# The experts' stage as one written stream of weight pieces, and six low parts moved from GpSimd to VectorE

## The chip, the cores and the metric

The kernel runs on one core of a Trainium2 chip. The metric is the device time of one execution in microseconds (us). A profiled execution also has a span, from its first to its last instruction.

Engines are named as in the profile: PE is TensorE's matmul, PEld its weight load, DVE is VectorE, ACT ScalarE, POOL GpSimd, SP SyncE. Each takes its instructions in order; SP and POOL also issue DMA transfers.

## The reference

The input of 1024 tokens of 1024 values goes through two blocks. The change lies in the first block's last part, a mixture of 16 experts in which each expert chooses its own tokens:

```python
def expert_choice_ffn(h, w_router, w_gate, w_up, w_down):
    cap = CAPACITY_FACTOR * seq // N_EXPERTS                 # 2 * 1024 // 16 = 128
    probs = softmax(einsum('bld,de->ble', h, w_router))
    gate, idx = lax.top_k(transpose(probs, (0, 2, 1)), cap)  # 128 tokens per expert
    xs = h[idx]                                              # (16, 128, 1024)
    a = einsum('becd,edf->becf', xs, w_gate)                 # w_gate, w_up: 16 x 1024 x 2048
    u = einsum('becd,edf->becf', xs, w_up)
    y = einsum('becf,efd->becd', silu(a) * u, w_down)        # w_down: 16 x 2048 x 1024
    y = y * gate[..., None]
    return segment_sum(y, idx)                               # added back to the tokens' rows
```

Before it stand a norm, a gated mixer and a state-space branch; after it a second block with attention, a recurrence and a last norm. All weights are float32.

## The kernel before

**Split products.** A float32 matrix product is made of three products in the fast float32 form. Each operand is split into a high part (a rounded copy) and a low part (what the copy leaves over), and `mm3` (L240) adds high x high, high x low and low x high. A weight piece is 128 rows of 1024 columns. `piece` (L1845) makes its high part on ScalarE (L1849) and its low part by a subtraction (L1853). The high parts are named wh and mh, the low parts wl and ml, for even and odd pieces; each name has three buffers, so there are six pairs. The subtraction runs on GpSimd for the first six pieces of the stage and on VectorE for all others. ScalarE's first six copies stand behind the router's last exponential (`k.route`).

**Loads.** `fetched` (L1825) loads two pieces, 1 MB, at a time, into a ring of large buffers (eight A, two pairs of wr, two mr; at the stage's start two more pairs, t and m). SP issues these loads, and a load waits until the low parts of the buffer's earlier content are made. The loads numbered 15 and 16 are issued by GpSimd, ordered behind the first gather of rows (`k.rows`).

**One expert.** `gather` (L1856) finds the expert's token numbers: VectorE compares slot numbers (the one-hot oh, L1859), eight small matmuls sum it, ScalarE and VectorE make the index (L1868, L1869; the first is `k.first`), and GpSimd fetches the 128 rows by an indirect DMA (L1876). `transposed` (L1882) turns the rows by TensorE (L228), and evicts them as a high part on ScalarE (L1890) and a low part on VectorE (L1891). The hidden width of 2048 is made in two halves, the units u = (expert, half). For a unit come three products of eight pieces: `gate`, `up` and `down`. A piece is six matmuls of 512 columns. `up` starts with the silu of the gate sums on ScalarE (L1925) and ends with the product of the two on VectorE (L1929). `flip` transposes that into the operand of `down`. After the second half's `down`, ScalarE scales the sums by the router's weight (L1949), and GpSimd adds the rows to the tokens by an indirect DMA that accumulates (L1950), the scatter. The last expert's rows are taken over by the second block instead (`k.tail`).

**Order.** The loop at the end of `moe` traces `up(u)`, `gate(u + 1)`, `down(u)` for each unit, with the index work of the next expert ahead of `up`, the transposes of its rows ahead of `up`'s seventh piece, and `flip(u)` ahead of `gate(u + 1)`'s seventh piece. Splits are traced just ahead of their matmuls. The program's compile-time planner then orders each engine's instructions: it plays the program through with estimated durations, and takes the first traced one among those it holds ready. `add_manual_dep` with ORDER adds an edge to this planning and no wait on the chip. In `_pe` (L230) such edges keep the matmuls that write one accumulation tile in their order. The router (`Router`, L1389) ends just ahead of the stage: a sort by eight maxima at a time (L1461, L1463), merges of sorted rows (L1487, L1488), a threshold, then the slots (L1551).

Of the kernel before, what the change touches and what calls it, by code (L numbers as in the profile page):

```python
# [13 lines left out]
OP = mybir.AluOpType  # L14
# [140 lines left out]
class K:  # L155
    def __init__(s, tc, ins, ctx):
        s.tc, s.nc, s.i, s.ctx = tc, tc.nc, ins, ctx
        s.pp = ctx.enter_context(tc.tile_pool(name="pp", bufs=8, space=PSUM))
        s.dp = ctx.enter_context(tc.tile_pool(name="dp", bufs=1, space=DRAM))
        s.base = ctx.enter_context(tc.tile_pool(name="base", bufs=1))  # L160
        s.pool = s.base
        s.n = 0
        s.spare = {}
        s.last = {}
        s.turn = False
        s.wait = None

    def nm(s, p):
        s.n += 1
# [60 lines left out]
    def _pe(s, out, x):  # L230
        n = out.tensor.name
        if n in s.last:
            s.tc.add_manual_dep(x.ins, s.last[n].ins.name, ORDER, reason="one group of a bank at a time")
        s.last[n] = x
        if s.wait:
            s.tc.add_manual_dep(x.ins, s.wait.ins.name, ORDER, reason="what is surely ready first")
            s.wait = None
        s.pe = x
# [1572 lines left out]
def moe(k, dbg=None):  # L1811
    nc, i, c = k.nc, k.i, k.c
    V, S, SY, GP = nc.vector, nc.scalar, nc.sync, nc.gpsimd
    dbg = dbg or {}
    ident = c("ident")
    PM = k.tc.tile_pool(name="PM", bufs=1)
    k.pool = PM.__enter__()
    NE, NF = 16, 2048
    cnt = [0]

    turns = ["A"] * 8 + ["wr"] * 2 + ["mr"] * 2
    first = ["A"] * 8 + ["t"] + ["wr"] * 2 + ["mr"] * 2 + ["m"]
    MH, AHEAD = 3, 2

    def fetched(src):  # L1825
        n = cnt[0] // 2

        q = first[n] if n < len(first) else turns[(n - len(first)) % len(turns)]
        if q in ("A", "mr"):
            z = k.a2(F32) if q == "A" else k.t([128, 2048], "mr", 2)  # L1830
            to = [(z, src)]
            got = [z[:, :1024], z[:, 1024:]]
        else:
            got = [k.wraw(), k.wraw()] if q == "wr" else [k.g("th"), k.g("tl")] if q == "t" else [k.m(5), k.m(4)]
            to = list(zip(got, (src[:, :1024], src[:, 1024:])))
        for z, x in to:
            if n in (len(first) + 1, len(first) + 2):

                x = GP.dma_start(z, x)
                k.tc.add_manual_dep(x.ins, k.rows.ins.name, ORDER, reason="the rows first")  # L1840
            else:
                SY.dma_start(z, x)
        return got

    def piece(raw):  # L1845
        n = cnt[0]
        cnt[0] += 1
        h, l = (k.g("wh", k.NH, FR, k.base), k.g("wl", k.NH, FR, k.base)) if n % 2 == 0 else (k.g("mh", MH, FR), k.g("ml", MH, FR))
        a = S.activation(h, raw, AF.Copy)  # L1849
        if n < 6:  # L1850

            k.tc.add_manual_dep(a.ins, k.route.ins.name, ORDER, reason="routing first")
        (GP if n < 6 else V).tensor_tensor(l, raw, h, op=OP.subtract)  # L1853
        return h, l

    def gather(e):  # L1856
# [3 lines left out]
        if e == 1:  # L1860
            k.tc.add_manual_dep(x.ins, k.first.ins.name, ORDER, reason="the first expert first")
# [6 lines left out]
        S.activation(a, p[:, 0:1], AF.Copy, scale=8.0)  # L1868
# [24 lines left out]

    def product(w, x, first, last, ps, before=None):

        for kk in range(8):
            if kk % 2 == 0:
                raw = fetched(w[kk // 2])
            wh, wl = piece(raw[kk % 2])
            if kk == 8 - AHEAD and before:  # L1900
                before()
            xs = slice(kk * 128, kk * 128 + 128)
            for h in range(2):
                hs = slice(h * 512, h * 512 + 512)
                k.mm3(ps[h], x[0][:, xs], x[1][:, xs], wh[:, hs], wl[:, hs], first and kk == 0, last and kk == 7)

    X, hid, G, Dn = {}, {}, {}, {}
    units = [(e, h) for e in range(NE) for h in range(2)]

    def fetch(e):  # L1910
        X[e] = gather(e)

    def turn(e):
        X[e] += (transposed(X[e][1], "x", 2),)

    def gate(u, before=None):
        e, h = units[u]
        G[u] = [k.ps("pa") for _ in range(2)]
        product(i["w_gate"][e, h], X[e][2], True, True, G[u], before)

    def up(u, before=None):
        e, h = units[u]
        g = k.m(2 + u % 2)
        for q in range(2):
            S.activation(g[:, q * 512:(q + 1) * 512], G[u][q], AF.Silu)  # L1925
        P = [k.ps("pa") for _ in range(2)]
        product(i["w_up"][e, h], X[e][2], True, True, P, before)
        for q in range(2):
            V.tensor_tensor(g[:, q * 512:(q + 1) * 512], g[:, q * 512:(q + 1) * 512], P[q], op=OP.mult)  # L1929
        hid[u] = g  # L1930

    def flip(u, tag="t"):
        hid[u] = transposed(hid[u], tag, 1 if tag == "t" else 2)

    def down(u):
        e, h = units[u]
        x = hid[u]
        if h == 0:
            Dn[e] = [k.ps("pb") for _ in range(2)]
        product(i["w_down"][e, h], x, h == 0, h == 1, Dn[e])  # L1940
        if h == 1:
            ix, xs, _ = X[e]
            if e == NE - 1:

                k.tail = ix, xs[:, 1024 + e:1025 + e], Dn[e]
                return
            y = k.m(4 + e % 2)
            for q in range(2):
                S.activation(y[:, q * 512:(q + 1) * 512], Dn[e][q], AF.Copy, scale=xs[:, 1024 + e:1025 + e])  # L1949
            GP.indirect_dma_start(out=k.acc[:, :], out_offset=bass.IndirectOffsetOnAxis(ap=ix[:, :1], axis=0),  # L1950
                                  in_=y, in_offset=None, compute_op=OP.add)

    fetch(0)
    turn(0)
    gate(0)
    n = len(units)
    for u in range(n - 1):
        e, h = units[u]
        if h == 0 and e + 1 < NE:
            fetch(e + 1)  # L1960

        up(u, (lambda: turn(e + 1)) if h == 1 and e + 1 < NE else None)
        gate(u + 1, lambda: flip(u))
        if u + 2 < n:
            down(u)
    up(n - 1)
    flip(n - 1, "x")
    down(n - 2)
    down(n - 1)
    PM.__exit__(None, None, None)  # L1970


# [22 lines left out]
```

## Time and profile before

| | us |
|---|---|
| median of 3 runs | 2871.28 (2870.67 to 2875.26) |
| the profiled execution | 2875.23 |
| its span | 2873.5 |
| PE busy | 2763.0 (96%) |
| PEld busy | 2253.5 (78%) |
| DVE busy | 2232.4 (78%) |
| ACT busy | 1618.4 (56%) |
| POOL busy | 138.4 (5%) |

Matmuls are pipelined and their ends are modelled, so a busy PE is not necessarily a PE at its peak. The starts of neighbouring matmuls tell more. Busy shares are means over stages with different limits. In a timeline row an instruction's start and duration stand first; what its engine waited for just before it stands in brackets at the end.

### The profile page before, as it was taken

Reading aid. Unit: us, or ns where it says so; the run is one execution under the profiler, and the core shown is the slowest. Engines: PE = TensorE matmul, PEld = TensorE weight load, DVE = VectorE, ACT = ScalarE, POOL = GpSimd, SP = SyncE. Lnnn points to the kernel's source line nnn. Section 1 sums busy time; section 2 is a strip of 40 time slices with the busy share of each in tenths; the row PEclk is TensorE's granted clock in tenths of the full one; section 3 lists DMA queues with packets and bytes.
Section 4 is the critical chain, followed back from the end, with each engine's and each line's share of the span. In section 5 each row is a group of like instructions: output and inputs, shape, how many; then the busy total and the mean of one; then the engine's idle time right before and its main releaser. Section 6 shows DMA issues by size and latency. Waiting matters only on the chain. (4 is left out here: it accounts for less than half of the span.)

```text
span 2873.5 us, 37166 instructions
## 1 busy us (share of the span) xinstructions
PE 2763.0 (96%) x13353; PEld 2253.5 (78%) x13353; DVE 2232.4 (78%) x3619; ACT 1618.4 (56%) x2205; POOL 138.4 (5%) x106
## 2 busy tenths in 40 slices
PE   8999999949999999999999998899999999999998
PEld 8889887738888877777777776688888788887877
DVE  7966476679999888888888888978888565568774
ACT  6343234228888777777777776546655344445531
POOL 0000000020000000000000001200000300000000
PEclk9999999979999999999999999899999999999999
DMA  7223465459999999999999996123334754457762
GB/s 257 67 75 96 132 215 187 169 195 339 375 379 375 354 364 365 365 364 364 366 364 365 365 367 212 54 105 112 114 129 143 232 152 161 158 203 261 259 202 81
DMA packets 181705, 678.18 MB, mean 236 GB/s; under 512 B 34960, under 2 KB 46352, under 8 KB 140816
## 3 DMA queue, kind: packets, MB, share of 16 engines
q1 hardware_dynamic: 176624, 656.80, 62.8%
q0 software_dynamic: 4896, 19.01, 2.6%
q8 instruction: 105, 1.72, 0.2%
q14 instruction: 80, 0.66, 0.1%
HBM read 588.01 MB, written 85.62 MB: 234 GB/s over the span
## 5 line engine op out<-in xcount | busy, mean ns | idle before, releaser
L225 PE MATMUL ps<-A,wh 128*128 128x512 f32 x1920 | 603.6, 395 | 4.5 <-DVE u L541 1.9
L225 PEld LDWEIGHTS ps<-A,wh 128*128 128x128 f32 x1920 | 357.1, 188 | 81.9 <-issue 2.6
L225 PE MATMUL ps<-A,wl 128*128 128x512 f32 x960 | 375.9, 392 | 0.0
L1853 DVE TENSOR_TENSOR wl<-A,wh 128x1024 fp32r<-128x1024 f32 x253 | 308.8, 1221 | 38.5 <-ACT wh L1849 36.9
L1853 DVE TENSOR_TENSOR ml<-A,mh 128x1024 fp32r<-128x1024 f32 x253 | 308.5, 1219 | 9.5 <-ACT mh L1849 3.1
L225 PE MATMUL ps<-S,wh 128*128 128x512 f32 x960 | 304.4, 398 | 5.5 <-DVE u L546 3.4
L1849 ACT ACTIVATE wh<-A 128x1024 fp32r<-128x1024 f32 x256 | 270.2, 1055 | 23.9 <-PE ps L225 23.9
L1849 ACT ACTIVATE mh<-A 128x1024 fp32r<-128x1024 f32 x256 | 270.0, 1055 | 21.2 <-PE ps L225 21.1
L219 ACT ACTIVATE wh<-wr 128x512 fp32r<-128x512 f32 (+2 forms) x168 | 154.8, 922 | 223.5 <-PE ps L225 174.4
L225 PE MATMUL ps<-wl,xh 128*128 128x512 f32 x520 | 209.1, 402 | 10.1 <-DVE wl L1853 10.1
L220 DVE TENSOR_TENSOR wl<-wr,wh 128x1024 fp32r<-128x1024 f32 (+2 forms) x166 | 175.4, 1056 | 53.1 <-ACT wh L219 38.4
L225 PEld LDWEIGHTS ps<-S,wh 128*128 128x128 f32 x960 | 178.9, 189 | 45.7 <-DVE u L546 5.1
L225 PEld LDWEIGHTS ps<-A,wl 128*128 128x128 f32 x960 | 180.2, 188 | 39.6 <-issue 0.7
L225 PE MATMUL ps<-wh,xl 128*128 128x512 f32 x520 | 205.3, 395 | 0.0
L225 PE MATMUL ps<-ml,xh 128*128 128x512 f32 x520 | 204.1, 393 | 0.5 <-DVE ml L1853 0.5
L225 PE MATMUL ps<-mh,xl 128*128 128x512 f32 x520 | 203.3, 391 | 0.0
L225 PE MATMUL ps<-S,wl 128*128 128x512 f32 x480 | 189.1, 394 | 0.0
L225 PE MATMUL ps<-wh,xh 128*128 128x512 f32 x520 | 188.2, 397 | 0.0
L225 PE MATMUL ps<-mh,xh 128*128 128x512 f32 x520 | 186.6, 393 | 0.2 <-ACT mh L1849 0.2
L225 PE MATMUL ps<-wh,A 128*128 128x256 f32 (+1 forms) x704 | 143.5, 299 | 8.7 <-ACT wh L219 8.7
L228 PE MATMUL ps<-sm,m 128*128 128x128 f32 (+1 forms) x692 | 102.4, 278 | 28.6 <-DVE m L1488 14.2
L225 PEld LDWEIGHTS ps<-wl,xh 128*128 128x128 f32 x520 | 97.9, 188 | 39.9 <-DVE wl L1853 18.5
(509 smaller groups left out, 5505.7 us busy)
## 6 DMA issues: line engine op xcount, KB each, us to landing
A<-in_w_up_dram SPq DMA_DIRECT2D x125, 1024.0 KB, 7.9
A<-in_w_down_dram SPq DMA_DIRECT2D x65, 1024.0 KB, 6.8
A<-in_w_gate_dram SPq DMA_DIRECT2D x64, 1024.0 KB, 6.6
wr<-in_w_gate_dram SPq DMA_DIRECT2D x124, 512.0 KB, 7.0
mr<-in_w_down_dram SPq DMA_DIRECT2D x59, 1024.0 KB, 7.0
wr<-in_w_in_dram SPq DMA_DIRECT2D x82, 512.0 KB, 4.2
wr<-in_w_mod_dram SPq DMA_DIRECT2D x24, 512.0 KB, 4.4
wr<-in_w_ing_dram SPq DMA_DIRECT2D x16, 512.0 KB, 4.6
```

The lines of the kernel that those rows point to most:

```text
L219: s.parts = (s.nc.scalar.activation(hi, raw, AF.Copy), (eng or s.nc.vector).tensor_tensor(lo, raw, hi, op=OP.subtract))
L220: (eng or s.nc.vector).tensor_tensor(lo, raw, hi, op=OP.subtract))
L225: s._pe(out, s.nc.tensor.matmul(out, a, b, start=start, stop=stop, skip_group_check=True))
L228: s._pe(out, s.nc.tensor.transpose(out, a, ident))
L1849: a = S.activation(h, raw, AF.Copy)
L1853: (GP if n < 6 else V).tensor_tensor(l, raw, h, op=OP.subtract)
```

## The change

One stream replaces the functions that called each other. `todo` lists the products of all units in the order of before, except that the last `flip` now stands inside `down(n - 2)`. For each of its 8 x 96 pieces N the stream traces first the split of piece N + 5, then what `plan` has put down for N, then the matmuls of N. `AHEAD` is 5 where it was 2; five splits are traced ahead of the first matmul.

- `plan` puts the silu of a gate at the first piece of the following product, the product of gate and up at the first piece of the product that follows `up`, its `flip` at that one's sixth piece, the scaling and scatter (`put`) at the first piece after the second `down`. The next expert's one-hot stands at the second piece, and its index and gather at the fifth piece, of the product that follows the first half's `gate`; the transposes of its rows stand at the sixth piece of the second half's `up`.
- `k.chain` makes each TensorE instruction of the stream follow the one traced before it.
- `behind` orders ScalarE's other instructions behind the newest high part (`k.hi`) and VectorE's behind the newest low part (`k.lo`).
- The first six low parts are made by VectorE, ordered behind the first expert's index (`k.first`). The one-hot of expert 1 loses its edge to that index.
- Loads 14, 15 and 16 go to GpSimd's queue behind the first gather, where 15 and 16 were.

```diff
+        if s.chain:
+            s.tc.add_manual_dep(x.ins, s.pe.ins.name, ORDER, reason="as they stand")
...
-    MH, AHEAD = 3, 2
+    MH, AHEAD = 3, 5
...
-            if n in (len(first) + 1, len(first) + 2):
+            if len(first) <= n < len(first) + 3:
...
-        a = S.activation(h, raw, AF.Copy)
+        k.hi = a = S.activation(h, raw, AF.Copy)
...
-        (GP if n < 6 else V).tensor_tensor(l, raw, h, op=OP.subtract)
+        x = V.tensor_tensor(l, raw, h, op=OP.subtract)
+        if n < 6:
+            k.tc.add_manual_dep(x.ins, k.first.ins.name, ORDER, reason="the first expert's rows are asked for")
+        k.lo = x
...
+    def behind(x, of):
+
+        if of:
+            k.tc.add_manual_dep(x.ins, of.ins.name, ORDER, reason="the parts first")
+        return x
...
-            S.activation(h[:, hs], p, AF.Copy)
-            V.tensor_tensor(l[:, hs], p, h[:, hs], op=OP.subtract)
+            behind(S.activation(h[:, hs], p, AF.Copy), k.hi)
+            behind(V.tensor_tensor(l[:, hs], p, h[:, hs], op=OP.subtract), k.lo)
...
+    for o, (what, u) in enumerate(todo):
         e, h = units[u]
+        if what == "gate":
+            plan(o + 1, 0, lambda u=u: silu(u))
+            if h == 0 and e + 1 < NE:
+                plan(o + 1, 1, lambda e=e: onehot(e + 1))
+                plan(o + 1, 4, lambda e=e: fetch(e + 1))
+        elif what == "up":
+            plan(o + 1, 0, lambda u=u: times(u))
+            plan(o + 1, 5, lambda u=u: flip(u, "x" if u == n - 1 else "t"))
+            if h == 1 and e + 1 < NE:
+                plan(o, 5, lambda e=e: turn(e + 1))
+        elif h == 1:
+            plan(o + 1, 0, lambda e=e: put(e))
...
+    onehot(0)
     fetch(0)
     turn(0)
+    k.chain = True
+    for N in range(AHEAD):
+        split(N)
+    for N in range(8 * len(todo)):
+        split(N + AHEAD)
+        for f in at.get(N, ()):
+            f()
...
+        for q in range(2):
+            hs = slice(q * 512, q * 512 + 512)
+            k.mm3(ps[q], x[0][:, xs], x[1][:, xs], wh[:, hs], wl[:, hs], opens and kk == 0, ends and kk == 7)
+    k.chain = False
```

## Rows read from the trace of the kernel before

**Rows 1.** Busy time by stretches: PE, PEld, DVE, ACT, POOL, PEclk, DMA share, GB/s.
```profile
630.00:640.00 10.00, 5.94 (x19) 4.80 (x20) 1.41 (x3) 2.26 (x3) 1.85 (x3) 0.52 0.68 263
850.00:950.00 100.00, 100.00 (x465) 81.51 (x465) 92.03 (x87) 79.80 (x87) 7.72 (x4) 1.00 0.99 377
...
1450.00:1550.00 100.00, 98.77 (x445) 78.36 (x443) 85.41 (x84) 71.93 (x82) 3.62 (x2) 1.00 0.96 370
```

**Rows 2.** Timeline of POOL: one gather, and the scatters of experts 0, 3, 4, 14.
```profile
651.34 1.02 POOL L1876 DMA_INDIRECT m<-h,ix  x1 [19.48 <-DVE ix L1869]
719.46 2.48 POOL L1950 DMA_INDIRECT acc<-m,ix  x1 [67.10 <-DVE wl L1853]
...
927.68 2.43 POOL L1950 DMA_INDIRECT acc<-m,ix  x1 [65.25 <-DVE wl L1853]
...
997.72 1.58 POOL L1950 DMA_INDIRECT acc<-m,ix  x1 [65.87 <-ACT m L1949]
...
1719.32 1.59 POOL L1950 DMA_INDIRECT acc<-m,ix  x1 [67.69 <-DMA A<-in_w_up_dram]
```

**Rows 3.** Timeline of all engines where up ends and gate begins, slow pace.
```profile
1115.90 1.28 DVE L1929 TENSOR_TENSOR m<-m,ps 128x512 f32<-128x512 f32 x2 [3.58 <-PE ps L225]
...
1116.64 1.25 PE L228 MATMUL ps<-sm,m 128*128 128x128 f32 x8
...
1117.34 1.19 ACT L1890 ACTIVATE th<-ps 128x512 fp32r<-128x512 f32 x2 [5.46 <-PE ps L228]
...
1118.38 0.51 PE L225 MATMUL ps<-wl,xh 128*128 128x512 f32 x1 [0.48 <-DVE wl L1853]
```

**Rows 4.** Timeline of PE around the same eight transposes, good pace.
```profile
807.02 0.40 PE L225 MATMUL ps<-mh,xl 128*128 128x512 f32 x1
807.25 1.03 PE L228 MATMUL ps<-sm,m 128*128 128x128 f32 x8
808.05 0.48 PE L225 MATMUL ps<-wh,xh 128*128 128x512 f32 x1
```

**Rows 5.** Timeline of POOL: the first and the last of six low parts.
```profile
597.60 3.23 POOL L1853 TENSOR_TENSOR wl<-A,wh 128x1024 fp32r<-128x1024 f32 x1 [301.77 <-PE ps L228]
...
609.99 2.33 POOL L1853 TENSOR_TENSOR ml<-A,mh 128x1024 fp32r<-128x1024 f32 x1
```

**Rows 6.** Timeline of DVE: merge steps of the router.
```profile
603.14 2.37 DVE L1488 TENSOR_TENSOR m<-m 16x64 f32<-16x64 f32 x1
...
610.30 2.10 DVE L1487 TENSOR_TENSOR m<-m 16x64 f32<-16x64 f32 x1
...
612.67 0.20 DVE L1487 TENSOR_TENSOR m<-m 16x64 f32<-16x64 f32 x1
```

**Rows 7.** Timelines of DVE, POOL and PE: first index, gather, transposes, first matmul.
```profile
628.37 0.15 DVE L1869 TENSOR_TENSOR ix<-ixa,ps 128x1 int32<-128x1 f32 x1 [0.67 <-ACT ixa L1868]
...
628.81 1.85 POOL L1876 DMA_INDIRECT m<-h,ix  x1 [16.49 <-DVE ix L1869]
...
634.06 1.97 PE L228 MATMUL ps<-sm,m 128*128 128x128 f32 x8 [5.93 <-DMA m<-h,ix]
635.87 0.79 PE L225 MATMUL ps<-wh,xh 128*128 128x512 f32 x1
```

**Rows 8.** SP's waits from 860 to 930 us; all transfers from 800 to 850.
```profile
SPq L1842 <- DVE ml L1853: 54.5, 25, 3.3
...
DMA packets 3313, 19.65 MB, mean 393 GB/s; under 512 B 372, under 2 KB 372, under 8 KB 1461
```

**Rows 9.** The page's costliest groups: busy us, mean ns, idle before.
```profile
L1853 DVE TENSOR_TENSOR wl<-A,wh 128x1024 fp32r<-128x1024 f32 x253 | 308.8, 1221 | 38.5 <-ACT wh L1849 36.9
...
L1849 ACT ACTIVATE wh<-A 128x1024 fp32r<-128x1024 f32 x256 | 270.2, 1055 | 23.9 <-PE ps L225 23.9
```

**Rows 10.** Timeline of PE: the first matmul after expert 14, the stage's last.
```profile
1718.03 0.62 PE L225 MATMUL ps<-wh,xh 128*128 128x512 f32 x2
...
1779.33 0.39 PE L225 MATMUL ps<-mh,xl 128*128 128x512 f32 x1
```

More of the change, by code (lines that the diff above doesn't have):

```diff
@@ L166, in __init__ @@
         s.wait = None
+        s.chain = False
     def nm(s, p):
@@ L1848, in piece, with onehot @@
         h, l = (k.g("wh", k.NH, FR, k.base), k.g("wl", k.NH, FR, k.base)) if n % 2 == 0 else (k.g("mh", MH, FR), k.g("ml", MH, FR))
-        a = S.activation(h, raw, AF.Copy)
+        k.hi = a = S.activation(h, raw, AF.Copy)
         if n < 6:
             k.tc.add_manual_dep(a.ins, k.route.ins.name, ORDER, reason="routing first")
-        (GP if n < 6 else V).tensor_tensor(l, raw, h, op=OP.subtract)
+        x = V.tensor_tensor(l, raw, h, op=OP.subtract)
+        if n < 6:
+            k.tc.add_manual_dep(x.ins, k.first.ins.name, ORDER, reason="the first expert's rows are asked for")
+        k.lo = x
         return h, l
-    def gather(e):
+    def behind(x, of):
+        if of:
+            k.tc.add_manual_dep(x.ins, of.ins.name, ORDER, reason="the parts first")
+        return x
+    k.hi = k.lo = None
+    OH = {}
+    def onehot(e):
         oh = k.t([128, 8, 128], "oh", 1, BF)
@@ L1859, in gather @@
         x = V.tensor_tensor(oh, bc(k.slots, 1, 8), bc(sl, 2, 128), op=OP.is_equal)
-        if e == 1:
-            k.tc.add_manual_dep(x.ins, k.first.ins.name, ORDER, reason="the first expert first")
+        behind(x, k.lo)
+        OH[e] = oh
+    def gather(e):
+        oh = OH.pop(e)
         p = k.ps("pb")
@@ L1867, in gather @@
         ix = k.t([128, 1], "ix", 3, I32) if e < NE - 1 else k.t([128, 1], "lix", 1, I32, k.base)
-        S.activation(a, p[:, 0:1], AF.Copy, scale=8.0)
+        behind(S.activation(a, p[:, 0:1], AF.Copy, scale=8.0), k.hi)
         x = V.tensor_tensor(ix, a, p[:, 1:2], op=OP.add)
@@ L1889, in transposed @@
             hs = slice(q * 512, q * 512 + 512)
-            S.activation(h[:, hs], p, AF.Copy)
-            V.tensor_tensor(l[:, hs], p, h[:, hs], op=OP.subtract)
+            behind(S.activation(h[:, hs], p, AF.Copy), k.hi)
+            behind(V.tensor_tensor(l[:, hs], p, h[:, hs], op=OP.subtract), k.lo)
         return h, l
[L1894 to L1905, printed above, removed]
@@ L1907, in moe, with turn, silu @@
     X, hid, G, Dn = {}, {}, {}, {}
     units = [(e, h) for e in range(NE) for h in range(2)]
+    n = len(units)
+    def turn(e):
+        X[e] += (transposed(X[e][1], "x", 2),)
     def fetch(e):
         X[e] = gather(e)
[L1913 to L1923, printed above, removed]
+    def silu(u):
+        hid[u] = k.m(2 + u % 2)
@@ L1924, in up, with times @@
         for q in range(2):
-            S.activation(g[:, q * 512:(q + 1) * 512], G[u][q], AF.Silu)
-        P = [k.ps("pa") for _ in range(2)]
-        product(i["w_up"][e, h], X[e][2], True, True, P, before)
+            behind(S.activation(hid[u][:, q * 512:(q + 1) * 512], G[u][q], AF.Silu), k.hi)
+    def times(u):
         for q in range(2):
-            V.tensor_tensor(g[:, q * 512:(q + 1) * 512], g[:, q * 512:(q + 1) * 512], P[q], op=OP.mult)
-        hid[u] = g
+            z = hid[u][:, q * 512:(q + 1) * 512]
+            behind(V.tensor_tensor(z, z, U[u][q], op=OP.mult), k.lo)
@@ L1932, in flip, with put @@
     def flip(u, tag="t"):
         hid[u] = transposed(hid[u], tag, 1 if tag == "t" else 2)
-    def down(u):
-        e, h = units[u]
[L1937 to L1951, printed above, removed]
+    def put(e):
+        ix, xs, _ = X[e]
+        if e == NE - 1:
+            k.tail = ix, xs[:, 1024 + e:1025 + e], Dn[e]
+            return
+        y = k.m(4 + e % 2)
+        for q in range(2):
+            behind(S.activation(y[:, q * 512:(q + 1) * 512], Dn[e][q], AF.Copy, scale=xs[:, 1024 + e:1025 + e]), k.hi)
+        GP.indirect_dma_start(out=k.acc[:, :], out_offset=bass.IndirectOffsetOnAxis(ap=ix[:, :1], axis=0),
+                              in_=y, in_offset=None, compute_op=OP.add)
@@ new lines, in moe, with plan @@
+    todo = [("gate", 0)]
+    for u in range(n - 1):
+        todo += [("up", u), ("gate", u + 1)] + [("down", u)] * (u + 2 < n)
+    todo += [("up", n - 1), ("down", n - 2), ("down", n - 1)]
+    at = {}
+    U = {}
+    def plan(o, kk, f):
+        at.setdefault(8 * o + kk, []).append(f)
+    for o, (what, u) in enumerate(todo):
+        e, h = units[u]
+        if what == "gate":
[10 more added lines that the diff above has]
+            plan(o + 1, 0, lambda e=e: put(e))
@@ new lines, in moe, with split, banks @@
+    parts = {}
+    def split(N):
+        if N >= 8 * len(todo):
+            return
+        what, u = todo[N // 8]
+        e, h = units[u]
+        kk = N % 8
+        if kk % 2 == 0:
+            parts["raw"] = fetched(i[{"gate": "w_gate", "up": "w_up", "down": "w_down"}[what]][e, h, kk // 2])
+        parts[N] = piece(parts["raw"][kk % 2])
+    def banks(what, u):
+        e, h = units[u]
+        if what == "down":
+            if h == 0:
+                Dn[e] = [k.ps("pb") for _ in range(2)]
+            return Dn[e]
+        p = [k.ps("pa") for _ in range(2)]
+        (G if what == "gate" else U)[u] = p
+        return p
@@ L1953, in moe @@
+    onehot(0)
     fetch(0)
     turn(0)
-    gate(0)
-    n = len(units)
-    for u in range(n - 1):
-        e, h = units[u]
[L1959 to L1969, printed above, removed]
+    k.chain = True
[5 more added lines that the diff above has]
+            f()
+        what, u = todo[N // 8]
+        e, h = units[u]
+        kk = N % 8
+        if kk == 0:
+            ps = banks(what, u)
+        x = hid[u] if what == "down" else X[e][2]
+        opens, ends = (h == 0, h == 1) if what == "down" else (True, True)
+        wh, wl = parts.pop(N)
+        xs = slice(kk * 128, kk * 128 + 128)
+        for q in range(2):
+            hs = slice(q * 512, q * 512 + 512)
+            k.mm3(ps[q], x[0][:, xs], x[1][:, xs], wh[:, hs], wl[:, hs], opens and kk == 0, ends and kk == 7)
@@ L1970, in moe @@
+    k.chain = False
+    for f in at.get(8 * len(todo), ()):
+        f()
     PM.__exit__(None, None, None)
```

## The prediction

> **What bounds the kernel now.** I read the slices of the page first. TensorE is busy in nine tenths or more of nearly every slice; the one hole is the slice near 600 us, where the router picks the tokens, and the experts' stage follows it, from about 636 to 1780 us. Three further views split these two stretches.
>
> The table by stretches [rows 1] shows that the experts' stage has two paces. From 850 to 950 us TensorE has no idle time and starts 465 matmuls; from 1450 to 1550 us it starts 445 (some records may be missing, so I use this only as a pointer). The line of GpSimd gives the exact pace, because each expert ends in one scatter [rows 2]: from expert 0 to expert 3 the scatters stand (927.68 - 719.46) / 3 = 69.4 us apart; from expert 4 to expert 14 they stand (1719.32 - 997.72) / 10 = 72.2 us apart. The work of an expert is the same throughout.
>
> What the slow pace loses is seen at the change of a product [rows 3]. VectorE reaches the product of gate and up (L1929) in its order early and sits 3.58 us until TensorE has finished the up sums; ScalarE sits 5.46 us at the eviction of the transposed hidden rows. Both engines do their work in order, so the splits of the next pieces queue behind these two waits. TensorE then runs out of split pieces: from the start of the eight transposes at 1116.64 to the next matmul at 1118.38 it needs 1.74 us. At the good pace [rows 4] the same eight transposes lie between two matmuls 1.03 us apart, one matmul being 0.23: 0.8 us. In the good stretch the stage is at TensorE's own limit: 288 matmuls of 0.23 us are 66.2, three groups of transposes 2.4, the rest is index work and rounding. No weight transfer is waited for: the loads wait for released buffers, 54.5 us out of a 70 us stretch [rows 8], so the ring of raw pieces stands full.
>
> In the router's hole the chain is VectorE's. GpSimd makes six lo parts there, from 597.60 to 612.3 [rows 5]. VectorE's merge steps of 16x64 elements take 2.37 and 2.10 us under them, and 0.20 once GpSimd is done [rows 6]; the last long one ends at 612.40, where GpSimd's last step ends at 612.32. Then the sort goes on, and after it come threshold, slots and the first index (628.37), the gather (628.81), its transposes (634.06) and the first matmul (635.87) [rows 7].
>
> **The change part by part.** *The six lo parts leave GpSimd.* The router's six stretched VectorE steps (one copy 1.92, merge steps 0.62, 2.37, 2.16, 2.37, 2.10; [rows 6] shows the second and the last merge step) have 11.5 us where 0.14 and five times 0.20 would do: 10.4 us. VectorE is busy nearly all of 597 to 621 us, so nearly all of it is on the path. Bounds: 8 if a row exchange through TensorE comes late instead, 10.4 at best. I take 10.4.
>
> *The six lo parts come to VectorE behind the first index.* Six at about 1.2 us each [rows 9], overlapping a little, are 6.9 us. They lie between the index and the first lo half of the gathered rows; the gap from 628.37 to the first matmul is 7.5 us [rows 7], and the one-hot of expert 1, which filled 1.2 us of it, moves out into the stream. So the gather hides them. Without this cover (all six ahead of the xl halves, and a quick gather) they cost up to one or two steps, 1.2 to 2.4 us. Queued behind them are xl and later lo parts; the first expert's second matmul waits for that. The gather is also issued while VectorE now works: an indirect issue takes 1.02 us beside an idle VectorE and up to 2.48 beside a busy one [rows 2], against 1.85 here before [rows 7]: a cost of 0 to 0.6. I take 0.5 in all.
>
> *One more fetch on GpSimd's queue* (number 14, from SP's). It is issued behind the first gather, some 0.6 us of GpSimd's time, and is used by pieces 28 and 29, and a piece is six matmuls, 6 x 0.23 = 1.38 us, so 39 us after the stage starts: nothing. SP's queue loses one entry that stood behind a wait. TensorE's clock stays as it was: the granted clock is 0.52 from 630 to 640 us, the 1.2 GHz level after an idle hole, and 1.00 in the stage [rows 1]; the hole becomes shorter and is still a hole.
>
> *The stream.* Five pieces of splits are traced ahead of the matmuls, TensorE's order is written out, and each silu, product, eviction and index step stands behind the newest split. There are six pairs of split buffers, so split N+5 starts when TensorE has finished piece N-1, that is when it starts N. Count from there, in the rows' own times. The hi half takes 1.05 us and the lo half 1.22 [rows 9], so lo N+5 is ready 2.3 us later and is due five pieces later, at 6.9 us. At a product change the product of gate and up (1.28 us, [rows 3]) ends after 3.6 us; the transposes that read it now stand five pieces in, 6.9 us: 3.3 us to spare. The evictions of the transposed rows (1.19 on ScalarE, about 1.3 on VectorE) end 3.6 us after the transposes start, and the down product that reads them comes three pieces and the transposes later, 4.9 us. ScalarE no longer reaches a wait on TensorE before the splits that TensorE needs, which was the mechanism of rows 3. VectorE's sum per expert, 48 lo parts 1.14 apart, ten half steps of about 0.64 and a one-hot of 1.2, is 62.3 of 69.4 us. So all experts run at the good pace.
>
> Experts 4 to 14: from the scatter at 927.68 to that at 1719.32 are 791.6 us for 11 experts; 11 x 69.4 is 763.4. Gain 28.2 us.
>
> The last part: from the start of the product behind the last scattered down (1718.03) to the last expert matmul (1779.33, [rows 10]) are 61.3 us for five products and two groups of transposes. At the good pace a product is (69.4 - 2.4 - 0.2) / 6 = 11.1 us, so 5 x 11.1 + 1.6 = 57.1, less the last matmul's own 0.23: gain 4.4 us.
>
> *Index and gather of the next expert* move four pieces later. The gathered rows are wanted three products later (over 30 us), and the gather stood behind the scatter on GpSimd's queue anyway: nothing. *The second block* is traced as before, but the compile-time order of its first instructions can shift; nothing bounds that better than a few us either way. I take 0 and allow 5.
>
> Sum: 10.4 - 0.5 + 28.2 + 4.4 = 42.5 us. The profiled execution took 2875.23 us with a span of 2873.5, so its like would be 2832.7. The median of the runs, 2871.28, lies 4 us under that execution; the gains come off it alike: **2829 us**.
>
> **The rivals.** *Transfers bind at the quicker pace.* At the good pace 377 GB/s were moved at a DMA share of 0.99 [rows 1]. The weights of an expert are 25.2 MB, gather and scatter add some 1.5 MB with the read for the accumulation: 26.7 / 377 is 70.9 us. If 377 were the ceiling, and the ring's lead spent by expert 4, twelve experts would lose 1.5 each: 18 us, 2847. Against it: 50 us of the same stretch ran at 393 GB/s, and SP waited for buffers in it, not the reverse [rows 8]. The Trainium skill (SBUF — State Buffer, "A bandwidth-pool intuition that's wrong") gives some 358 GB/s from HBM to a core; by that figure an expert's 26.7 MB would need 74.6 us, an estimate from that page, the experts would gain nothing and the result would be near 2861. The trace's 377 and 393 GB/s are above the figure, and the measurement decides.
>
> *Lo parts in the gather's way.* If the gather's issue stayed shut out until the six are made, the start would come up to 6.9 us later: 2836. The issue of 2.48 us in the middle of uninterrupted lo parts speaks against it [rows 2]. The Trainium skill (SBUF — State Buffer, "Who interferes with whom") has a steady two-input VectorE step shut out GpSimd's reads but infers that descriptor writing goes on; the row agrees but for about a microsecond.
>
> *The change doesn't do what it says.* The order of VectorE is held only from one side (behind a split, not ahead of the next), so a wait could still stand ahead of a needed split. Then only the router's gain stays: 2861.
>
> *Slower.* The rigid order of TensorE makes it wait where it could go past. Place: the transposes at the sixth piece, behind the product of gate and up, behind split N+5. If VectorE enters the change with k lo parts unmade, that product ends at 3.6 + 1.14 k and TensorE waits for all beyond 6.9, at each of 32 units. From k = 4 on, 1.3 us each, 41 us, it eats the whole gain; at k = 5 it is 2.4 x 32 = 76 us, net 34 slower, 2905. Against it: at the good pace VectorE is busy 92 of 100 us [rows 1] and TensorE never waits.
>
> **How the numbers follow.** Forecast 0.72 (2822 to 2838 by its own bounds: 2 us of the router, 2 of the lo parts, 5 of the second block); gather shut out 0.09 (2836); transfers 0.06 (2847); order not held 0.07 (2861); TensorE waiting 0.06, of which 0.04 slower, 0.01 within, 0.01 faster. The range 2821 to 2841 holds the first two and a part of the third. A difference of about 0.2% (5.7 us) is what a measurement of this kernel can tell from no change; faster than that has 0.72 + 0.09 + 0.06 + 0.07 + 0.01 = 0.95, within 0.01, slower 0.04; I move 0.02 to the middle for mishaps I can't name: 0.93, 0.03, 0.04.
>
> **What would show it.** Right: no lo part on GpSimd's line, merge steps of 0.2 us in the router, the first expert matmul near 626 us; scatters 69.4 us apart from first to last, transposes always between two matmuls about a microsecond apart; ScalarE idle some 0.3 us per piece on TensorE's buffers and VectorE no longer seconds behind L1929's sums; the last expert matmul near 1737 us. Wrong: scatters that drift apart with SP no longer waiting for buffers (transfers); a long first gather issue (lo parts); idle TensorE ahead of transposes, released by the product of gate and up (rigid order); a second block that takes another time than the 1094 us from 1779 to the end of the span.

## The result, and the profile after

The changed kernel takes 2834.91 us, the median of 4 runs (2829.15 to 2838.36); the kernel before took 2870.98 us beside it (4 runs, 2869.92 to 2875.26). The ratio is 0.987, its 95% interval 0.985 to 0.9889. One of the seven runs of the experiment that moves the low parts alone took 6135.52 us where the others took 2859.49 to 2865.78, and its numbers leave it out. The forecast was 2829 with a range of 2821 to 2841. The profiled execution took 2836.0 us with a span of 2834.2, that of before 2875.23 with 2873.5: 39.2 us less.

The engines' sums hardly moved, but GpSimd lost its six parts. From the page, busy time by engine:

```profile
PE 2745.6 (97%) x13353; PEld 2259.5 (80%) x13353; DVE 2245.5 (79%) x3625; ACT 1656.7 (58%) x2205; POOL 113.7 (4%) x101
```

The table by stretches answers to [rows 1] (PE, PEld, DVE, ACT, POOL, granted clock, DMA share, GB/s). Both stretches now look alike, with no idle time on TensorE and VectorE at 92 of 100:

```profile
850.00:950.00 100.00, 100.00 (x458) 81.64 (x457) 91.94 (x86) 81.97 (x89) 6.16 (x4) 1.00 1.00 383
1450.00:1550.00 100.00, 100.00 (x465) 81.46 (x464) 92.38 (x88) 81.66 (x90) 6.10 (x4) 1.00 0.97 368
```

GpSimd's timeline, the scatters of experts 0, 13 and 14, answers to [rows 2]:

```profile
714.81 2.15 POOL L1945 DMA_INDIRECT acc<-m,ix  x1 [0.30 <-issue]
...
1617.39 2.10 POOL L1945 DMA_INDIRECT acc<-m,ix  x1 [0.30 <-issue]
1685.16 1.56 POOL L1945 DMA_INDIRECT acc<-m,ix  x1 [65.68 <-DMA A<-in_w_down_dram]
```

(1617.39 - 714.81) / 13 = 69.4 us: the good pace from the first expert to the last. The last scatter stands 67.8 us behind the one before; no gather is issued ahead of it, which is some 1.3 us of the difference. A scatter also comes later after its expert's sums than before, so the stage is measured by matmuls below.

The change of a product, which was [rows 3]. VectorE's product of gate and up comes without a wait, and the transposes that read it start 4.50 us after it, with ScalarE's copies behind them, without a wait:

```profile
1140.93 1.28 DVE L1930 TENSOR_TENSOR m<-m,ps 128x512 f32<-128x512 f32 x2
...
1145.43 1.03 PE L229 MATMUL ps<-sm,m 128*128 128x128 f32 x8
1146.59 1.07 ACT L1908 ACTIVATE th<-ps 128x512 fp32r<-128x512 f32 x2
```

In the router's hole the last exponential (ScalarE's timeline before, then after), the merge steps of [rows 6], and the first index, the gather, transposes and first matmul of [rows 7] (timelines of VectorE, GpSimd and TensorE):

```profile
596.12 0.36 ACT L1438 ACTIVATE P<-ps,smx,h2ry 128x16 f32<-128x16 f32 x1 [1.70 <-DVE smx L1437]
```
```profile
597.30 0.36 ACT L1441 ACTIVATE P<-ps,smx,h2ry 128x16 f32<-128x16 f32 x1 [1.70 <-DVE smx L1440]
```
```profile
602.11 0.20 DVE L1490 TENSOR_TENSOR m<-m 16x64 f32<-16x64 f32 x1
...
619.28 0.15 DVE L1887 TENSOR_TENSOR ix<-ixa,ps 128x1 int32<-128x1 f32 x1 [0.67 <-ACT ixa L1886]
619.35 1.22 DVE L1856 TENSOR_TENSOR wl<-A,wh 128x1024 fp32r<-128x1024 f32 x1
```
```profile
619.73 1.85 POOL L1894 DMA_INDIRECT m<-h,ix  x1 [322.38 <-DVE ix L1887]
```
```profile
624.84 1.97 PE L229 MATMUL ps<-sm,m 128*128 128x128 f32 x8 [5.80 <-DMA m<-h,ix]
626.64 0.79 PE L226 MATMUL ps<-wh,xh 128*128 128x512 f32 x1
...
1682.47 0.40 PE L226 MATMUL ps<-wh,xh 128*128 128x512 f32 x1
...
1739.35 0.39 PE L226 MATMUL ps<-mh,xl 128*128 128x512 f32 x1
```

The last two rows answer to [rows 10]. The 39.2 us split as follows; each length lies between two instructions of the same kind in both traces.

| stretch | before | after | gain | forecast |
|---|---|---|---|---|
| start to the router's last exponential | 596.12 | 597.30 | -1.2 | 0 |
| exponential to first index | 32.25 | 21.98 | 10.3 | 10.4 |
| index to first expert matmul | 7.50 | 7.36 | 0.1 | -0.5 |
| first matmul to the product behind the last scattered down | 1082.16 | 1055.83 | 26.3 | 28.2 |
| from there to the last expert matmul | 61.30 | 56.88 | 4.4 | 4.4 |
| last expert matmul to the end of the span | 1094.17 | 1094.85 | -0.7 | 0 |

In the fourth stretch one new wait appears. It is the only one that the list of waits shows for a matmul between 630 and 1725 us. The timelines of ScalarE, VectorE and TensorE at this place:

```profile
640.87 1.28 ACT L1925 ACT_TABLE_LOAD   x1
642.17 1.09 ACT L1925 ACTIVATE m<-ps 128x512 f32<-128x512 f32 x2
643.14 1.06 ACT L1852 ACTIVATE wh<-A 128x1024 fp32r<-128x1024 f32 x1
```
```profile
644.23 1.22 DVE L1856 TENSOR_TENSOR wl<-A,wh 128x1024 fp32r<-128x1024 f32 x1 [2.12 <-ACT wh L1852]
645.38 1.22 DVE L1874 TENSOR_TENSOR oh<-sr,slotT 128x1024 bf16<-128x1024 bf16 x1
```
```profile
644.90 0.39 PE L226 MATMUL ps<-mh,xl 128*128 128x512 f32 x1
646.65 0.35 PE L226 MATMUL ps<-sr,oh 128*128 128x2 bf16 x8 [1.36 <-DVE oh L1874]
```

Read it from the first row down: the first silu loads its table (1.28 us) in ScalarE's order, the high part behind it comes late, VectorE waits 2.12 us for it, the one-hot of expert 1 stands behind that low part, and TensorE, whose order is written out, waits 1.36 us for the one-hot.

### The profile page after: what moved, and what is told of

The parts are those of the page before. It is cut to its first block, busy times and chain, and to the rows that moved or that the text cites. A ratio compares the mean times of both kernels' runs of the same rounds, so it can differ in the third digit from the quotient of the medians.

```text
span 2834.2 us, 37263 instructions
## 1 busy us (share of the span) xinstructions
PE 2745.6 (97%) x13353; PEld 2259.5 (80%) x13353; DVE 2245.5 (79%) x3625; ACT 1656.7 (58%) x2205; POOL 113.7 (4%) x101
## 5 line engine op out<-in xcount | busy, mean ns | idle before, releaser
L1852 ACT ACTIVATE wh<-A 128x1024 fp32r<-128x1024 f32 x256 | 272.1, 1063 | 67.3 <-PE ps L226 65.5
L226 PEld LDWEIGHTS ps<-A,wl 128*128 128x128 f32 x960 | 180.3, 188 | 39.8 <-issue 0.7
L226 PE MATMUL ps<-mh,xh 128*128 128x512 f32 x520 | 207.7, 399 | 0.0
L226 PE MATMUL ps<-wh,xh 128*128 128x512 f32 x520 | 205.3, 395 | 0.0
L226 PEld LDWEIGHTS ps<-wh,A 128*128 128x128 f32 x704 | 113.3, 194 | 14.2 <-ACT wh L220 9.3
L405 DVE TENSOR_TENSOR st<-u,ps 128x512 f32<-128x512 f32 x96 | 76.8, 800 | 56.2 <-PE ps L226 54.3
```

The source lines that it names most:

```text
L226: s._pe(out, s.nc.tensor.matmul(out, a, b, start=start, stop=stop, skip_group_check=True))
L405: V.tensor_tensor(o, a, b, op=ADD)
L1852: k.hi = a = S.activation(h, raw, AF.Copy)
```

## The experiments

The theory was that two gains add up that have nothing to do with each other: the router's (GpSimd's parts beside VectorE's steps) and the stage's (other work of ScalarE and VectorE queued ahead of needed splits). The rivals were that the transfers or the written order of TensorE, not the order of the splits, make the pace. All changes are against the changed kernel, but for the second. Of the changed kernel itself there are two medians, taken on separate occasions: 2834.91 and 2833.35 us.

### Each half alone

The six low parts back on GpSimd:

```diff
-        x = V.tensor_tensor(l, raw, h, op=OP.subtract)
-        if n < 6:
-            k.tc.add_manual_dep(x.ins, k.first.ins.name, ORDER, ...)
-        k.lo = x
+        x = (GP if n < 6 else V).tensor_tensor(l, raw, h, op=OP.subtract)
+        k.lo = x if n >= 6 else None
```

> The kernel after, with the first six low parts back on GpSimd. Two independent gains (theory): only the router's gain goes. VectorE's merge steps stretch again beside GpSimd's low parts, about 10 us in all; the first index comes about 10 us later than the 619.3 us of the kernel after; the scatters stay 69.4 us apart; total 2835 + 10 = 2845 us. Rival (the stretched steps only filled time in which VectorE would have waited for a row exchange anyway): the steps stretch, the index comes less than 4 us later, total under 2839.

Measured: 2844.77 us, ratio 0.9888 (0.9865 to 0.9911). From the last exponential to the first index it is 32.26 us, as before's 32.25. The scatters stay 69.4 apart, and first to last expert matmul is 634.80 to 1746.72, 1111.9 us (before 1143.5, after 1112.7). Timelines of GpSimd and VectorE in the hole of this kernel:

```profile
609.48 2.33 POOL L1856 TENSOR_TENSOR ml<-A,mh 128x1024 fp32r<-128x1024 f32 x1
```
```profile
609.79 2.10 DVE L1490 TENSOR_TENSOR m<-m 16x64 f32<-16x64 f32 x1
611.82 0.20 DVE L1491 TENSOR_TENSOR m<-m 16x64 f32<-16x64 f32 x1
```

The merge step that meets GpSimd's last part ends with it, at 611.89 against 611.81; the next one takes 0.20.

The kernel before with the low parts' move alone:

```diff
-        (GP if n < 6 else V).tensor_tensor(l, raw, h, op=OP.subtract)
+        x = V.tensor_tensor(l, raw, h, op=OP.subtract)
+        if n < 6:
+            k.tc.add_manual_dep(x.ins, k.first.ins.name, ORDER, ...)
```

> The kernel before, with the six low parts moved to VectorE behind the first index and nothing else. Two independent gains: the first matmul of the experts' stage comes about 9 to 10 us earlier, the scatters keep their two paces (69.4 us up to expert 3, then 72.2), total 2871 - 10 = 2861 us. Rival (the pace of the stage depends on how it starts): the slow pace begins at another expert or goes away, total under 2850.

Measured: 2861.00 us, ratio 0.9958 (0.9943 to 0.9972). Exponential to index is 22.08 us; the stage keeps its two paces (69.4, then 72.2) and its length, 623.40 to 1766.26, 1142.9 us. The halves gain 29.3 and 13.1 us on the kernel before, which took 2874.05 us beside them, together 42.3, where the whole change gained 36.1 and, measured again, 39.8 (2873.19 less 2833.35): no more than the sum of its halves.

### What holds the low parts back

```diff
-        if n < 6:
-            k.tc.add_manual_dep(x.ins, k.first.ins.name, ORDER, ...)
```

> The kernel after with the six low parts on VectorE but not held behind the first index. Theory (VectorE is the router's bound): they fall among the router's last steps, as soon as their high parts are there, and put six times 1.14 us into its chain: index 6.9 us later than held, total 2835 + 7 = 2842 us. Rival (VectorE has room between the router's dependent steps): under 2 us later, 2836 us.

Measured: 2839.06 us, ratio 0.9877 (0.9861 to 0.9894). Now VectorE makes all six inside the router, five of them from 604.30 to 610.95. VectorE's timeline of this kernel:

```profile
604.30 1.20 DVE L1856 TENSOR_TENSOR ml<-A,mh 128x1024 fp32r<-128x1024 f32 x1
...
624.11 0.15 DVE L1885 TENSOR_TENSOR ix<-ixa,ps 128x1 int32<-128x1 f32 x1 [0.67 <-ACT ixa L1884]
```

Exponential to index is 28.08 us, 6.1 longer than with the edge, and exponential to first matmul 34.8 against 29.3. So the six parts cost about their own length ahead of the index.

Behind it they cost far less, but not nothing. In this kernel and in the one with the parts on GpSimd, VectorE has no work between the first index and the gathered rows, and the first gather's issue takes 1.13 us where it takes 1.85 in the changed kernel. GpSimd's and VectorE's timelines of this kernel, then GpSimd's of the one with the parts on GpSimd:

```profile
624.56 1.13 POOL L1892 DMA_INDIRECT m<-h,ix  x1 [328.29 <-DVE ix L1885]
```
```profile
630.79 0.69 DVE L1907 TENSOR_TENSOR xl<-ps,xh 128x512 fp32r<-128x512 f32 x1 [6.53 <-ACT xh L1906]
```
```profile
628.31 1.13 POOL L1892 DMA_INDIRECT m<-h,ix  x1 [16.50 <-DVE ix L1885]
```

From index to first matmul it is 6.71 us here and 6.93 with the parts on GpSimd, against 7.36 in the changed kernel: 0.4 to 0.65 us.

### Which part of the stream is needed

TensorE's written order taken away:

```diff
-    k.chain = True
+    k.chain = False
```

> The kernel after without the written order of TensorE; ScalarE's and VectorE's orders stay what they are. If the splits' lead on ScalarE and VectorE is what keeps TensorE fed: scatters 69.4 us apart within 0.3, total 2835 us within 4. Rival (TensorE's written order carries the gain): matmuls with high parts are taken ahead and low parts are waited for again, scatters up to 72.2 apart in the later experts, total up to 2863 us.

Measured: 2831.86 us, ratio 0.985 (0.9829 to 0.9872); 69.4 us per expert, no wait for the one-hot, first to last matmul 1110.1 us. The written order gains nothing.

The edges of ScalarE and VectorE taken away:

```diff
     def behind(x, of):
-        if of:
-            k.tc.add_manual_dep(x.ins, of.ins.name, ORDER, reason="the parts first")
         return x
```

> The kernel after without the edges that hold ScalarE's and VectorE's other steps behind the newest split; TensorE's written order stays. In the later experts the silu then stands four splits earlier in ScalarE's order and the evictions three. Theory (a wait ahead of needed splits is what costs): behind the silu's wait the second next high part comes 2.2 us after the product change and its low part 3.4, due at 2.8: 0.6 us of idle TensorE per silu and per scaled output, some 2 us per expert from the expert on at which the planned order turns, so 15 to 30 us, total 2850 to 2865 us. Rival (the written order of TensorE and five traced splits do it alone): scatters 69.4 apart, total 2835 us.

Measured: 2856.61 us, ratio 0.9937 (0.9916 to 0.9958). The scatters stand 69.4, 69.4, 70.2 and 67.3 us apart, then 71.3. More than half of the gain is lost: 1.0 us in the router, where the one-hot of expert 1 now stands ahead of the first index (exponential to index 23.02 us), and nearly all of the rest from expert 4 on, with the splits still traced five pieces ahead. Timelines of VectorE and TensorE at one of the places of this kernel:

```profile
1211.64 0.69 DVE L1928 TENSOR_TENSOR m<-m,ps 128x512 f32<-128x512 f32 x1 [2.07 <-PE ps L226]
1212.24 1.22 DVE L1856 TENSOR_TENSOR wl<-A,wh 128x1024 fp32r<-128x1024 f32 x1
```
```profile
1212.12 0.40 PE L226 MATMUL ps<-wh,xh 128*128 128x512 f32 x1
1213.52 0.50 PE L226 MATMUL ps<-wl,xh 128*128 128x512 f32 x1 [1.00 <-DVE wl L1856]
```

VectorE sits 2.07 us at the product of gate and up, the low part behind it starts only then, and the matmul that reads it comes 1.40 us after the one before where 0.23 is usual. It is the mechanism of [rows 3], back once per expert. Eleven such stalls, 1.17 us each beyond the usual step, are some 13 of the 20.9 us by which the stage is longer than in the changed kernel (1133.6 against 1112.7); no row here names the rest. The waits from 640 to 1735 us (total us, times, longest), where the changed kernel has one wait of 1.4 for a matmul and none for th:

```profile
ACT th L1906 <- PE ps L229: 79.6, 23, 3.6
...
DVE m L1928 <- PE ps L226: 25.0, 12, 2.3
...
PE ps L226 <- DVE wl L1856: 11.0, 11, 1.0
```

### How far ahead

```diff
-    MH, AHEAD = 3, 5
+    MH, AHEAD = 3, 2
```

> The kernel after with two pieces of splits traced ahead instead of five; all edges stay. Theory (only the lead left behind a wait counts): behind the silu, split N+3's high part ends 2.2 us after the product change and its low part 3.4, due at 4.1; behind the transposes' evictions the low part ends at 4.0, due at 4.9: no idle TensorE, scatters 69.4 us apart, total 2835 us within 5. Rival (a lead of five is needed, for ScalarE's and VectorE's backlogs add up): back toward the slow pace, scatters 71 to 72.2 apart, total 2860 to 2876 us.

Measured: 2829.23 us, ratio 0.9845 (0.9828 to 0.9861); 69.4 us per expert, no wait of a matmul in the stage, 1110.8 us from first to last matmul. The waits of this kernel from 640 to 1735 us:

```profile
ACT th L1908 <- PE ps L229: 78.7, 23, 3.5
...
DVE m L1930 <- PE ps L226: 1.1, 1, 1.1
```

ScalarE sits at the evictions of the transposed rows as long as in the kernel without the edges (79.6 us), and TensorE doesn't notice. So a wait of ScalarE on TensorE costs nothing by itself; it costs where too few splits stand finished when the wait begins. VectorE's waits at the product of gate and up, 25.0 us without the edges, are nearly gone.

```diff
-    MH, AHEAD = 3, 5
+    MH, AHEAD = 3, 1
```

> The kernel after with one piece of splits traced ahead. Theory: behind the silu the low part of piece N+2 ends at 3.4 us and is due at 2.8: TensorE idle 0.65 us; behind a scaled output 0.75; behind the evictions of a flip or of an expert's rows 0.35. Per expert 2 x 0.65 + 0.75 + 3 x 0.35 = 3.1 us, scatters about 72.5 apart, 15 x 3.1 = 46 us, total about 2880 us. Rival (the written order helps at any lead): scatters 69.4 apart, 2835 us.

Measured: 2851.98 us, ratio 0.9924 (0.9907 to 0.994). The pace is 69.4 for three experts, 70.9 once, and 71.5 from then on: the expected direction, but 2.1 us per expert. TensorE's waits from 640 to 1735 us:

```profile
PE ps L226 <- DVE ml L1856: 6.0, 10, 0.6
...
PE ps L226 <- DVE wl L1856: 2.0, 11, 0.2
```

These waits are 8.0 of the 19.4 us by which the stage is longer than in the changed kernel (1132.1 against 1112.7); no row here names the rest. One piece of lead is too little, two are enough, and five bring nothing more.

### Transfers, and the next bound

The third matmul of each product is left out, so that TensorE needs a third less while all weights are still loaded and split (the output is not the reference's).

```diff
-            k.mm3(ps[q], x[0][:, xs], x[1][:, xs], wh[:, hs], wl[:, hs], ...)
+            k.mm(ps[q], x[0][:, xs], wh[:, hs], start=opens and kk == 0, stop=False)
+            k.mm(ps[q], x[0][:, xs], wl[:, hs], start=False, stop=ends and kk == 7)
```

> The kernel after with the third matmul (low x high) of each split product left out in the experts' stage, so that TensorE has a third less to do there; all loads and splits stay. It shows the next bound. Theory (TensorE bounds the stage, transfers have room): scatters come closer than 69.4 us; VectorE needs 62.3 us per expert, and 26.7 MB per expert at the best rate seen over 50 us, 393 GB/s, 68 us, at the 426 GB/s of single slices 63; so 63 to 68 us. Rival (transfers are the bound already, at 377 GB/s): scatters stay at 69.4 or above.

Measured: 2729.55 us in a single profiled run. The scatters stand 62.6 and 63.6 us apart by turns, 63.1 on average (704.50 to 1524.77, 13 spacings, without the last). The stretches of this kernel (columns as above):

```profile
1000.00:1100.00 100.00, 85.35 (x353) 61.13 (x351) 97.62 (x96) 84.67 (x98) 6.15 (x4) 0.93 1.02 409
1100.00:1200.00 100.00, 83.79 (x349) 57.85 (x350) 99.21 (x97) 83.84 (x95) 3.08 (x2) 0.96 1.02 414
```

The queues move 409 to 414 GB/s where the changed kernel needs 368 to 383, so the transfers don't bind at 69.4 us per expert. VectorE is at 98 of 100, and the 63.1 us lie beside the 62.3 that the prediction added up for it: it is the next bound. The waits of this kernel from 700 to 1600 us speak against the transfers as the bound here too:

```profile
DVE wl L1856 <- ACT wh L1852: 13.6, 22, 0.9
DVE ml L1856 <- ACT mh L1852: 0.5, 2, 0.4
```
```profile
ACT wh L1852 <- DMA mr<-in_w_down_dram: 9.9, 11, 3.2
```

VectorE waits for ScalarE alone, 14.1 us in 900, and never for a transfer. ScalarE's waits for transfers are 24.3 us in all. So even if every wait of VectorE came from a late transfer, transfers would cost some 1 us per expert. The granted clock of 0.93 and 0.96 is a mean: once per expert it stands at the 1.2 GHz level for some microseconds, beside TensorE's wait of 3.58 us for the next one-hot (0.50 from 1072 to 1078 us, for one).

### The one-hot of expert 1

```diff
-                plan(o + 1, 1, lambda e=e: onehot(e + 1))
+                plan(*((o, 4) if e == 0 else (o + 1, 1)), lambda e=e: onehot(e + 1))
```

> The kernel after, with the one-hot of the second expert moved from the second piece of the second product to the fifth piece of the first. Theory (it stood on VectorE behind a low part that waited for ScalarE's table load and silu): the stall of 1.4 us goes and nothing else changes, from the first to the last matmul 1111.3 us, total 1.4 us below the kernel after, which the times can hardly show. Rival (the index matmuls wait for something else): the stall stays.

Measured: 2834.98 us, ratio 0.9865 (0.985 to 0.988). The wait of 1.36 us is gone, and first to last matmul is 623.03 to 1732.96, 1109.9 us, 2.8 shorter than in the changed kernel. Only about half of that is the wait. The other half is, by estimate, TensorE's clock, which comes back sooner after the hole in this profile: over the six us from the first matmul on the mean granted clock is 0.90 here and 0.67 in the changed kernel, so some 1.2 us stand at the 1.2 GHz level here and 4.0 there. Matmuls start 0.43 us apart at that level and 0.23 apart at the upper one, which makes 1.3 us of the difference (from the rows of the timeline: 628.08 to 628.51 and 631.31 to 631.54 in the changed kernel). The six us of the changed kernel, then of this one:

```profile
626.64:632.64 6.00, 6.00 (x19) 4.76 (x19) 3.72 (x4) 2.72 (x3) 0.53 (x1) 0.67 0.86 307
```
```profile
623.03:629.03 6.00, 6.00 (x25) 4.86 (x25) 4.95 (x5) 3.68 (x4) 0.53 (x1) 0.90 0.88 302
```

The time as a whole doesn't show it: in this profile the second block took 1101 us where the other profiles show 1091 to 1098.

### The best two versions again

The changed kernel as it stands:

> The kernel after once more, as the measure for the three others. Its single stall of 1.4 us ahead of the second expert's index matmuls comes back, from the first to the last matmul of the experts' stage 1112.7 us, total 2832 to 2836 us.

Measured: 2833.35 us, ratio 0.9859 (0.9844 to 0.9874); first to last matmul 1112.2 us, the wait of 1.4 us is there again.

Two pieces ahead:

> Two pieces of splits traced ahead instead of five, beside the kernel after on the same chip. Theory (two are as good; five only brought the table load and the silu behind more splits): first to last matmul 1110.8 us, 1.9 us below the kernel after, total 2830 us. Rival (the lower time of the first run was the chip's or the day's): total equal to the kernel after within 1 us and the same length of the stage.

Measured: 2829.38 us, ratio 0.9847 (0.9833 to 0.9861); 1109.6 us.

Two pieces ahead, and TensorE's order not written out (`k.chain = False`):

> Two pieces ahead and no written order of TensorE. Theory (only the edges behind the splits are needed, with a lead of two or more): scatters 69.4 apart, total equal to that with two pieces and the written order within 2 us. Rival (with a lead of two the written order is what holds): low parts are waited for again, scatters above 70 apart, total above 2840 us.

Measured: 2830.36 us, ratio 0.9854 (0.9839 to 0.9869); 1110.2 us.

The nine profiles at the good pace with all matmuls part by the wait for the one-hot: the four with it need 1111.9 to 1112.7 us from first to last matmul, the five without it 1109.6 to 1110.8. The clock's rise blurs this, as its mean over the first six us is anything from 0.63 to 0.90. With its share taken off as above (an estimate), the groups stand clearer:

| profiles | first to last matmul | less the clock's share |
|---|---|---|
| five pieces ahead, with the wait (4) | 1111.9 to 1112.7 | 1110.9 |
| five pieces ahead, without it (2) | 1109.9 to 1110.1 | 1109.2 to 1109.4 |
| two pieces ahead, without it (3) | 1109.6 to 1110.8 | 1108.6 to 1108.8 |

So the wait costs about 1.6 us by this reckoning (1.36 by its row), and two pieces instead of five gain another 0.6, whose place no row here shows. In the times, two pieces ahead stand 4.0 us below the changed kernel where both were run side by side (2829.38 and 2833.35), and 5.7 below between the other two medians (2829.23 and 2834.91); the intervals of the ratios overlap, so the step in the profile is seen and the one in the time is not settled.

## Why the prediction was right, point by point

- **What bounds the kernel.** Right. With the edges of `behind` the slow pace is gone; without them most of it is back (71.3 us per expert, where it was 72.2), with VectorE's wait at the product of gate and up ahead of a needed low part. ScalarE's waits, which the prediction named beside it, matter only at too small a lead: with two pieces they are as long, 78.7 us, and the pace is 69.4.
- **The router.** 10.3 us against 10.4; the runs with the parts on GpSimd and off it give 32.26 and 22.08 us.
- **The low parts behind the index.** I took 0.5 us against the kernel before, and the stretch from index to first matmul became 0.1 shorter. That doesn't make the parts free: in the kernel before, the one-hot of expert 1 filled VectorE there, and the gather's issue took 1.85 us as it does now. Against the two kernels in which VectorE is idle there, with an issue of 1.13 us, the parts cost 0.4 to 0.65 us. So 0.5 us is their price against an idle VectorE; against the kernel before nothing was left to pay, because the one-hot stood there with the same issue of 1.85 us. The prediction's bound set a gather beside an idle VectorE (1.02 us) against a scatter beside a busy one (2.48), two kinds of transfer. The rival in which they shut the gather out until all six are made is false: the transposes start 5.56 us after the index, and 5.69 in the kernel before. Five of six parts are made by 625.1 us, a quarter of a microsecond after the transposes start, and the sixth (628.08) stands behind both xl halves and delays no matmul by a wait that the trace shows. The cover by the gather is shown by its loss: the unheld parts cost 6.1 us.
- **The stream.** 26.3 us against 28.2 for experts 4 to 14. The failing step is "all experts run at the good pace", with no price for the start of the stream. 1.36 us are the wait for expert 1's one-hot. The prediction counted the one-hot as 1.2 us that leave the gap ahead of the first matmul, and didn't ask what they meet in the stream, where the first silu's table load had made VectorE late. The remaining 0.5 us fit a pace that is 0.03 per expert slower, 69.43 against 69.40.
- **The reason for the stream's gain.** The prediction gave three things together: lead, written order, edges. Within the new stream, the edges with a lead of two pieces are enough. All runs but the second keep the rest of the stream (the places that `plan` gives, the later index work), and no run put the edges alone into the kernel before, so what these places add is not shown. The written order is not needed, and with five pieces of lead its price is the 1.36 us, as TensorE can't take other matmuls ahead of the late index work. This is the mechanism of the rival called slower, once instead of 32 times.
- **The last part.** 4.4 us against 4.4.
- **Transfers.** The rival is false by 409 to 414 GB/s. The Trainium skill (SBUF — State Buffer, "A bandwidth-pool intuition that's wrong"), with its 358 GB/s from HBM to a core, is contradicted as a ceiling for this one core by this run more than by the rows of before.
- **From the sum to the median.** The steps sum to 41.2 us in the profile where 42.5 were forecast. First and second block took another 1.9 us; the exponential starts anywhere between 593.6 and 597.3 us in kernels whose first block is the same, so this is run-to-run drift. The last 2.9 us come from taking the gains off the median: the profiled execution lay 4.0 us above it before, and 1.1 above it after.

What stays open is why the planned order turns bad at expert 4 and not earlier. It does so in the kernel before, without the edges, and at a lead of one. The planner works with estimated durations, and no run was made on these.

## What to carry to other kernels

In an engine that works in order, a step that waits for the slowest engine must stand behind the prefetches which that engine will need next. See to that by edges between these two kinds of step; here two pieces of lead were then as good as five, and one was too few. A helper engine's work in an idle hole isn't free if its steps shut out those of the critical engine: move it behind the step that starts a long transfer, where it cost about half a microsecond here instead of 6 to 10. When an order is written out by hand, look at its first round separately, where tables are loaded and buffers are still empty.

## What the runs showed of the hardware

- **The clock's rise.** After the hole the same matmuls run at a granted clock of 0.50, the 1.2 GHz level, for different times. In the changed kernel the first matmul stands at 626.64, and the clock is still 0.50 from 628 to 630 us; with the one-hot moved, whose work up to there is the same, the first matmul stands at 623.03 and the clock is 0.96 from 624 to 626. Matmuls that start 0.43 us apart at 0.50 start 0.23 apart at 1.00, so two profiles of the same stage can differ by over 1 us by this alone. The stretch of the changed kernel, then of the other:

```profile
628.00:630.00 2.00, 2.00 (x6) 1.52 (x5) 1.29 (x2) 0.35 (x1) 0.16 (x1) 0.50 0.95 356
```
```profile
624.00:626.00 2.00, 2.00 (x10) 1.63 (x10) 1.69 (x2) 0.70 (x1) 0.00 (x0) 0.96 0.80 254
```

- **Indirect issues.** The first gather's issue took 1.13 us where VectorE had nothing to do and 1.85 where it worked on a one-hot or on low parts, but for the kernel without the edges: there it took 1.25 and began 1.03 us after the index instead of 0.44 or 0.45. Later gathers took 0.98 us amid VectorE's stream of low parts (at 1060.68), the scatter right behind one 2.09 (at 1061.96), and the last scatter, with no gather ahead of it, 1.56. So VectorE's load is one part of it, and the kind of transfer and what went before it are others, which no run tells apart.
